# Seven quarter products for nine pairs of a gated MLP's up projection, with GpSimd forming the sums of the weights

## The chip, the cores and the metric

The kernel runs on one core of a Trainium2 chip. The metric is the device time of one execution in microseconds (us), lower is better. The engines are named as the profile names them: PE (TensorE, matrix products), DVE (VectorE), ACT (ScalarE), POOL (GpSimd) and SP (SyncE, which here only issues transfers). SBUF is the on-chip memory, PSUM the eight banks into which PE writes.

## The reference, cut to what matters

One layer of a streaming encoder over 512 tokens of width 1024: four parallel token mixers merged by gates, cross-attention into 256 memory tokens, then a gated MLP, each part between two RMS norms and added to the residual stream. All is float32. The change lies in the MLP (and in where the residual waits meanwhile):

```python
hf = _rms_norm(x, norm_ffn_pre)                       # 512 x 1024
u = _dwconv_causal(hf @ w_up, ffn_dw) + ffn_dw_b      # 512 x 5632, causal width 3 along the tokens
u_g, u_v = split(u, 2)                                # 2816 gate columns, 2816 value columns
yff = (silu(u_g) * u_v) @ w_down                      # 512 x 1024
x = x + _rms_norm(yff, norm_ffn_post)
```

## The kernel before

Every matrix product is made of three passes in a reduced float32 format. An operand is split into a high part (a cast by ACT) and a low part (operand minus high part, a subtraction by DVE); `mm3` (L239) then issues high x high, high x low and low x high into the same PSUM bank. `split_weights` (L179) does the split of a block of weights: the cast `wh` (L190, ACT) and the difference `wl` (L191, DVE). `run_blocks` (L203) takes the jobs of all stages in one line and fetches the weights three jobs ahead: the load by SP into `wr` (two buffers), then cast and difference into four buffers each. The order of the instructions on each engine is then set by the compiler's scheduler, under the waits that tiles and banks impose; each engine works its own queue in that order, and the issue of a transfer stands in the queue of the engine that issues it.

**The up projection** is `up_jobs` (L1550). There are 22 pairs j of 128 gate columns and 128 value columns. A product of 128 columns with all 512 tokens takes eight blocks of 128 input channels, three passes each: 24 matmuls with 512 columns. The tokens' operand is the tile pair `hth`, `htl`. The first four products (pairs 0 and 1) are done in two halves of 256 tokens, so that they can begin before the last tokens are normalised. After each product, ACT starts the causal convolution (`Identity` with bias and scale, L1557) and DVE adds the two other taps (L594, twice per product, one of its operands in PSUM). After the value product the gate is applied: tanh on ACT (L1561), then two operations of DVE (L1562, L1564) that write the pair's result into `quart`, the store of activations for the down projection.

**The down projection** is `down_jobs` (L1599). It already is Strassen's scheme with seven quarter products: rows of `w_down` are taken in 11 groups of two 128-row blocks, and phase 0 forms the products M1, M6, M5, M7, phase 1 the products M2, M3, M4. The sums of the weights are made while the up projection runs: `Sums` (L527) loads the rows on ACT's queue (L538), forms four sums on DVE (L542 to L545), and stores the result to DRAM on ACT's queue (L549); the down projection loads it from there (`load_parts`, L561, on SP's queue). The sums of the activations are four operations of POOL per group of two pairs (L566 to L569), issued in the up projection as soon as the second pair of the group is done, so that the down projection finds them ready.

**The residual.** `norm_task` (L1290) writes the residual of each 128 tokens into `ns.out[t]`, four tiles `res0` to `res3` of 128 x 1024 that stay in SBUF until `finish` (L1704) adds the MLP's normed result.

Of the kernel before, what the change touches and what calls it, by code (L numbers as in the profile page):

```python
# [17 lines left out]
F32 = mybir.dt.float32  # L18
# [65 lines left out]
def hybrid_layer(ctx: ExitStack, tc: tile.TileContext, a: dict, out: bass.AP):  # L84
# [146 lines left out]
    def matmul(ps, lhs, rhs, start, stop):  # L231
        PE.matmul(ps, lhs, rhs, start=start, stop=stop)  # L232
        bg.clock += max(int(math.prod(rhs.shape[1:])), 256) * 0.00042
# [293 lines left out]
    class Sums:  # L527


        def __init__(self, w, pairs, tile, queue, name):  # L530
            self.w, self.tile, self.queue, self.held = w, tile, queue, {}
            self.pairs, self.dram = pairs, dram.tile([pairs * P, 2 * D], F32, name=name)
# [7 lines left out]
        def add(self, q):  # L540
# [3 lines left out]
            V.tensor_tensor(b11, b22, b11, ALU.add)  # L544
            V.tensor_tensor(b21, b21, b11, ALU.subtract)  # L545
# [578 lines left out]
    def then(f):  # L1124

        return None, None, f
# [163 lines left out]
    def norm_task(t, ms, scaled, src, gain, act):  # L1290
# [17 lines left out]
    def open_mix_out():  # L1308
        close(m2)
        ns.res_, resp = new_pool("res", False)  # L1310
        ns.xr, ns.normed = None, []
        ns.out = [resp.tile([P, D], F32, name=f"res{t}") for t in range(NT)]
# [191 lines left out]
    def open_cross_out():  # L1504
# [5 lines left out]
        ns.hf = new_ht()  # L1510

# [26 lines left out]
    def open_ffn():  # L1538
# [6 lines left out]
        ns.quart = [(ns.fp.tile([P, 4, S // 2], F32, tag=f"qa{q}", name="qa"),  # L1545
                     ns.fp.tile([P, 3, S // 2], F32, tag=f"qb{q}", name="qb")) for q in range(NF // 2)]
        ns.post = ns.fp.tile([P, D], F32, name="g_ffn")
        G.dma_start(ns.post, a["norm_ffn_post"][0].partition_broadcast(P))

    def up_jobs():  # L1550
        st, held = {}, []

        def done(j, i, ps):
            if i == 0:
                st[j] = ns.fp.tile([P, 2, S], F32, tag="c", name="c", bufs=2)
            c, ch = st[j], i * NF + j
            st["first"] = A.activation(c[:, i], ps, AF.Identity, bias=pc("fb", ch), scale=pc("fdw2", ch)).ins  # L1557
            st["taps"] = taps(c[:, i], ps, lambda k: pc("fdw01", k * 44 + ch), 3).ins
            if i == 1:
                th = ns.fp.tile([P, S], F32, tag="th", name="th")  # L1560
                A.activation(th, c[:, 0], AF.Tanh, scale=0.5)  # L1561
                V.scalar_tensor_tensor(th, th, 1.0, c[:, 0], ALU.add, ALU.mult)  # L1562
                x = ns.quart[j // 2]
                V.scalar_tensor_tensor(x[j % 2][:, 0:2].rearrange("p a b -> p (a b)"), th, 0.5, c[:, 1],  # L1564
                                       ALU.mult, ALU.mult)
                if j % 2:
                    activation_sums(*x, G)


        for n in range(2 * NF):  # L1570
            def body(hi, lo, n=n):
                j, i = divmod(n, 2)
                if n > 3:
                    ps = bank()
                    channel_major(ps, (hi, lo), ns.hf)
                    done(j, i, ps)

                    q = n // 3 - 2
                    if 0 <= q < NF // 2:
                        with tc.issue_after(st["taps" if n % 3 == 0 else "first"]):  # L1580
                            (ns.sums.add, ns.sums.store, ns.sums.load)[n % 3](q + 2 * (n % 3 == 2))
                    return
                if n == 0:
                    bg.drain("n0")
                ps = bank(("mm", "sc")[n % 2])
                (channel_major if n else by_pass)(ps, (hi, lo), ns.hf, slice(0, S // 2))
                held.append((j, i, ps, (hi, lo)))
                if n == 3:
                    open_ffn()
# [230 lines left out]
```

## Time and profile before

| what | value |
|---|---|
| median of 3 runs | 1057.53 us (1055.94 to 1058.54) |
| the profiled execution's own time | 1055.79 us |
| its span in the profile | 1054.0 us, so 1.79 us lie around it |
| stage of the up projection | about 696 to 938 us of the span |
| stage of the down projection | about 938 us to the end |
| mean granted TensorE clock | 0.997 |

The profile shows one execution. Its page gives the busy time of each engine, the chain of work that ended last, and groups of instructions by line; the trace behind it can also be asked for the busy time of each engine in a stretch (windows) and for all instructions in order of time (timeline). In a timeline a line reads: start, duration, engine, line of the kernel, operation, output<-inputs, partitions x elements and count; a bracket at its end gives the idle time of the engine before it and what ended it. PE's matmuls overlap each other, so their spacing, not their duration, is what each costs.

### The profile page before, as it was taken

How to read it: one execution, taken by the hardware profiler on the slowest of the kernel's cores; microseconds unless marked ns; L12 is line 12 of the kernel's file. 1: busy time of each engine (PE TensorE's matmuls, PEld its weight loads, DVE VectorE, ACT ScalarE, POOL GpSimd, SP SyncE). 2: the span in 40 equal slices, each digit the busy share in tenths (PEclk: the TensorE clock that was granted, in tenths of full speed). 3: DMA queues.
4: the chain of work that ended last, by engine and by line, in shares of the span. 5: the costliest groups of instructions: out<-in, count | busy, mean ns of one | idle time of the engine just before them, and what ended most of it. 6: DMA issues, size and time to landing. Idle time of an engine off the chain costs nothing.

```text
span 1054.0 us, 14559 instructions
## 1 busy us (share of the span) xinstructions
PE 1041.7 (99%) x5295; PEld 886.8 (84%) x5295; DVE 807.1 (77%) x1280; ACT 501.9 (48%) x823; POOL 184.3 (17%) x309
## 2 busy tenths in 40 slices
PE   9999999999999999999999999999999999999996
PEld 8888888888888988888888899998888888888885
DVE  6899997668667467867487798777878777777795
ACT  5322222277465365655444566554333333355661
POOL 4000000300231233433011031121112111111001
PEclk9999999999999999999999999999999999999998
DMA  8854434742342353232359644135576676626662
GB/s 276 282 168 102 103 100 142 193 109 81 116 140 82 100 161 101 80 100 85 96 172 284 207 132 126 60 111 190 186 243 229 214 233 215 196 81 211 210 188 80
DMA packets 165373, 163.08 MB, mean 155 GB/s; under 512 B 6527, under 2 KB 136172, under 8 KB 165045
## 3 DMA queue, kind: packets, MB, share of 16 engines
q1 hardware_dynamic: 152995, 119.91, 38.0%
q0 software_dynamic: 5824, 19.03, 6.2%
q10 hardware_dynamic: 6482, 23.21, 5.7%
q8 instruction: 42, 0.69, 0.3%
q14 instruction: 30, 0.25, 0.1%
HBM read 139.03 MB, written 23.09 MB: 154 GB/s over the span
## 4 chain that ended last, share of the span: by engine, by line
PE 99%; DVE 0%; ACT 0%; issue 0%; POOL 0%; POOLq 0%; DVEq 0%; ACTq 0%
PE ps_mm L232 51%; PE ps_av L232 31%; PE ps_sc L232 8%; PE ps_tr L232 4%; PE ps_tr L236 2%; PE ps_mm L442 1%; PE ps_av L442 1%; PE ps_mm L384 0%; PE ps_sc L389 0%; DVE o L1710 0%; PE ps_tr L426 0%; POOL st_m L270 0%; POOLq L1816 0%; ACT hth L155 0%; ACT hth L432 0%
## 5 line engine op out<-in xcount | busy, mean ns | idle before, releaser
L190 ACT CAST wh<-wr 128x1024 fp32r<-128x1024 f32 (+1 forms) x142 | 148.8, 1049 | 273.3 <-PE ps_mm L232 175.0
L191 DVE TENSOR_TENSOR wl<-wr,wh 128x1024 fp32r<-128x1024 f32 (+1 forms) x142 | 178.5, 1258 | 79.0 <-ACT wh L190 78.8
L232 PE MATMUL ps_mm<-hth,wh 128*128 128x512 f32 (+1 forms) x592 | 221.1, 380 | 0.2 <-ACT hth L155 0.2
L232 PE MATMUL ps_mm<-htl,wh 128*128 128x512 f32 (+1 forms) x592 | 220.7, 379 | 0.0
L232 PE MATMUL ps_mm<-hth,wl 128*128 128x512 f32 (+1 forms) x592 | 220.6, 379 | 0.0
L232 PE MATMUL ps_av<-htl,wh 128*128 128x512 f32 (+1 forms) x352 | 131.8, 374 | 0.0
L232 PE MATMUL ps_av<-hth,wh 128*128 128x512 f32 (+1 forms) x352 | 131.8, 374 | 0.0
L232 PE MATMUL ps_av<-hth,wl 128*128 128x512 f32 (+1 forms) x352 | 131.6, 374 | 0.0
L232 PEld LDWEIGHTS ps_mm<-hth,wh 128*128 128x128 f32 x592 | 109.6, 188 | 20.4 <-ACT hth L155 0.8
L232 PEld LDWEIGHTS ps_mm<-hth,wl 128*128 128x128 f32 x592 | 109.5, 188 | 20.1
L232 PEld LDWEIGHTS ps_mm<-htl,wh 128*128 128x128 f32 x592 | 109.6, 188 | 19.7
L665 DVE SCALAR_TENSOR_TENSOR y<-y,par,y 128x482 f32<-128x482 f32 (+29 forms) x120 | 83.3, 735 | 0.1
L232 PEld LDWEIGHTS ps_av<-hth,wl 128*128 128x128 f32 x352 | 66.1, 188 | 11.9
L232 PEld LDWEIGHTS ps_av<-hth,wh 128*128 128x128 f32 x352 | 66.2, 188 | 11.8
L232 PEld LDWEIGHTS ps_av<-htl,wh 128*128 128x128 f32 x352 | 66.0, 188 | 11.7
L1613 DVE TENSOR_TENSOR wl<-dw,wh 128x1024 fp32r<-128x1024 f32 x32 | 40.2, 1262 | 13.3 <-ACT wh L1612 13.1
L1612 ACT CAST wh<-dw 128x1024 fp32r<-128x1024 f32 x32 | 33.4, 1051 | 23.4 <-PE ps_tr L232 7.9
L1058 POOL TENSOR_SCALAR fbias<-ck,cq 128x128 f32<-128x128 f32 (+3 forms) x32 | 28.2, 888 | 63.0 <-DVE st L1065 59.7
L1561 ACT ACTIVATE th<-c 128x512 f32<-128x512 f32 x22 | 13.9, 632 | 48.0 <-DVE c L594 48.0
L155 ACT CAST pth<-ps_tr 128x512 fp32r<-128x512 f32 (+3 forms) x56 | 23.5, 448 | 24.7 <-PE ps_tr L236 24.6
L594 DVE SCALAR_TENSOR_TENSOR c<-ps_mm,par,c 128x510 f32<-128x510 f32 (+1 forms) x44 | 32.8, 744 | 0.7
L156 DVE TENSOR_TENSOR ptl<-ps_tr,pth 128x512 fp32r<-128x512 f32 (+3 forms) x56 | 27.5, 512 | 5.9 <-ACT pth L155 5.4
(493 smaller groups left out, 2132.5 us busy)
## 6 DMA issues: line engine op xcount, KB each, us to landing
wr<-in_w_up SPq DMA_DIRECT2D x44, 512.0 KB
wr<-in_w_in SPq DMA_DIRECT2D x38, 512.0 KB
wr<-in_w_gate SPq DMA_DIRECT2D x32, 512.0 KB
wp<-in_w_down ACTq DMA_DIRECT2D x22, 512.0 KB
sums<-wp ACTq DMA_DIRECT2D x22, 512.0 KB
dw<-sums SPq DMA_DIRECT2D x44, 256.0 KB
wr<-in_w_branch SPq DMA_DIRECT2D x16, 512.0 KB
wide<-in_w_out SPq DMA_DIRECT2D x12, 512.0 KB
```

Of the source, the lines that this page charges most:

```text
L155: A.copy(hi, ps)
L156: V.tensor_tensor(lo, ps, hi.bitcast(F32), ALU.subtract)
L190: order(A.copy(hi, raw[:, :n]))
L191: low.tensor_tensor(lo, raw[:, :n], hi.bitcast(F32), ALU.subtract)
L232: PE.matmul(ps, lhs, rhs, start=start, stop=stop)
L236: PE.transpose(ps, x, ident[:n, :n])
L442: keep(PE.matmul(banks[c][:, :S // 2], w[p == 1][:, k, c * P:(c + 1) * P], ht[p == 2][:, i * 4 + k, :S // 2], start=(i, p, k) == (0, 0, 0) ...
L594: ins = V.scalar_tensor_tensor(dst[:, s:], src[:, :S - s], w(k), dst[:, s:], ALU.mult, ALU.add)
L665: ins = V.scalar_tensor_tensor(dst[:, s:], src[:, :S - s], pc("conv_dw", k * 4 + j), dst[:, s:], ALU.mult, ALU.add)
L1058: G.tensor_scalar(bias[:, :w], ck[j][:, :w], -1.0, cq[:, qt, head:head + 1], ALU.mult, ALU.add)
L1612: A.copy(hi, x)
L1613: V.tensor_tensor(lo, x, hi.bitcast(F32), ALU.subtract)
```

## The change

Nine of the 22 pairs (j = 4, 6, ..., 20) are computed by seven quarter products. For such a pair the matrix of [gate; value] weights (2 x 128 columns by 2 x 512 channels) is cut into four quarters, and so is the operand of the tokens (2 x 512 channels by 2 x 256 tokens). Each quarter product is four blocks of 128 channels, three passes, 256 token columns: 12 matmuls with 256 columns, 84 per pair in place of 48 with 512. Their results are combined in PSUM where the scheme allows (`x` takes A11, S2, S1 and S4 in turn, read out between them by ACT copies) and by three additions of DVE into a new tile `u`; convolution and gate then read `u` from SBUF.

- `token_terms`: once, POOL forms the four sums of the token operand's quarters, eight operations of 128 x 1024 (four add the high and low parts together again, four combine); ACT and DVE split them (`t0` to `t7`).
- `first_weights`: per pair, POOL forms four sums of weights of 128 x 512 (`su` twice, `wv` in place, `s4`). `load_pair` brings the raw weights one pair ahead into a ring of seven 128 x 1024 tiles, tag `dw`, which is shared with the tiles of `Sums` and, later, the down projection's loads. Three blocks of 128 x 1024 and one of 128 x 512 are split per pair, where it was two of 128 x 1024.
- The PE work of a pair j by seven products is laid between the halves of the plain pair j + 1, on the bank tags `sc` (two banks, for `x` and `v`) and `tr`.
- `Sums`: the last two of its four sums go to POOL (L544, L545 with `self.last`); its steps are taken by `step`, at most four per two pairs.
- The gate: `Silu` on ACT and one multiplication on DVE, in place of tanh and two operations.
- The sums of the activations move from the up projection to the down projection (`activation_terms`, POOL, three operations of 128 x 256 per group in phase 0 and one in phase 1), because `quart` now has room for the four plain quarters only; their splits become two instructions per part where they were one. The tiles that they use (`t6`, `t7`) are those of the token terms of the product A22.
- The residual is also stored to DRAM (`kept`, one transfer per 128 tokens on SP's queue), its SBUF tiles are used for token terms, and it is loaded again in `reload` at the third group of phase 0, together with the norm's gain (`ns.post`).

```diff
-            V.tensor_tensor(b11, b22, b11, ALU.add)
-            V.tensor_tensor(b21, b21, b11, ALU.subtract)
+            self.last.tensor_tensor(b11, b22, b11, ALU.add)
+            self.last.tensor_tensor(b21, b21, b11, ALU.subtract)
...
+        else:
+            SP.dma_start(ns.kept[t * P:(t + 1) * P, :], ns.out[t])
...
+    def ring(dtype=F32, name="dw"):
+        return ns.fp.tile([P, D], dtype, tag="dw", name=name, bufs=7)
+
+    def token_terms():
+        tok = [slice(i * S // 2, (i + 1) * S // 2) for i in range(2)]
+        b = {}
+        for k, t in ((0, 0), (0, 1), (1, 1), (1, 0)):
+            ks = slice(4 * k, 4 * k + 4)
+            x = b[k, t] = ring(name="b").rearrange("p (k c) -> p k c", k=4)
+            G.tensor_tensor(x, ns.hf[0][:, ks, tok[t]].bitcast(F32), ns.hf[1][:, ks, tok[t]].bitcast(F32), ALU.add)
+            if (k, t) == (0, 1):
+                G.tensor_tensor(b[0, 0], x, b[0, 0], ALU.subtract)
+            elif (k, t) == (1, 1):
+                G.tensor_tensor(b[0, 1], x, b[0, 1], ALU.subtract)
+                G.tensor_tensor(x, x, b[0, 0], ALU.subtract)
+            elif (k, t) == (1, 0):
+                G.tensor_tensor(x, x, b[1, 1], ALU.subtract)
+        for i, n in ((0, (0, 0)), (1, (1, 1)), (2, (0, 1)), (3, (1, 0))):
+            split(b[n], *ns.terms[i])
...
-                A.activation(th, c[:, 0], AF.Tanh, scale=0.5)
-                V.scalar_tensor_tensor(th, th, 1.0, c[:, 0], ALU.add, ALU.mult)
...
+            A.activation(c[:, 0], c[:, 0], AF.Silu)
+            V.tensor_tensor(ns.quart[j // 2][:, j % 2 * 2:j % 2 * 2 + 2].rearrange("p a b -> p (a b)"), c[:, 0],
+                            c[:, 1], ALU.mult)
...
+        seven = range(4, NF, 2)
...
+            def product(ps, name, b, first=True):
+                hi, lo = w[name]
+                for k in range(4):
+                    for i, (w_p, x_p) in enumerate(((hi, b[0]), (hi, b[1]), (lo, b[0]))):
+                        matmul(ps[:, :S // 2], w_p[:, k], x_p[:, k], first and i == k == 0, i == 2 and k == 3,
+                               not first)
+            def add(dst, ps):
+                V.tensor_tensor(dst, dst, ps[:, :S // 2], ALU.add)
+            def first_weights():
+                g, v = raws[j]
+                su, s4 = kept["su"], kept["s4"] = ring(name="su"), ns.fp.tile([P, S], F32, tag="s4", name="s4")
+                G.tensor_tensor(su[:, :S], v[:, :S], v[:, S:], ALU.add)
+                G.tensor_tensor(su[:, S:], su[:, :S], g[:, :S], ALU.subtract)
+                G.tensor_tensor(v[:, :S], g[:, :S], v[:, :S], ALU.subtract)
+                G.tensor_tensor(s4, g[:, S:], su[:, S:], ALU.subtract)
+                weights(("A11", "A12"), g)
+                return [()]
+            def second_weights():
+                load_pair(j + 2)
+                weights(("S1", "S2"), kept["su"])
+                return [()]
+            def third_weights():
+                weights(("S3", "A22"), raws.pop(j)[1])
...
+                split(kept["s4"], hi, lo)
...
+            def third(_):
+                u = kept["u"]
+                product(x["v"], "S3", ns.terms[2])
+                half_sums(*x["n"], range(4, NK))
+                done(n, 0, x["n"][0])
+                product(x["x"], "S1", ns.terms[0], False)
+                A.copy(u[:, 1, 1], x["x"][:, :S // 2])
+                add(u[:, 1, 1], x["v"])
+                step()
+            def value(hi, lo):
+                u, ps = kept["u"], bank()
+                half_sums(ps, (hi, lo), range(4))
+                product(x["x"], "S4", old(1, 1), False)
+                A.copy(u[:, 0, 1], x["x"][:, :S // 2])
+                half_sums(ps, (hi, lo), range(4, NK))
+                done(n, 1, ps)
+                step()
+                product(x["v"], "A22", ns.terms[3], False)
+                add(u[:, 1, 0], x["v"])
+                c = ns.fp.tile([P, 2, S], F32, tag="c", name="c", bufs=2)
+                for i in range(2):
+                    first_and_taps(c, j, i, u[:, i].rearrange("p a b -> p (a b)"))
+                gated(c, j)
+                step()
...
+        def reload():
+            ns.out = [term_tile(t).rearrange("p a b -> p (a b)") for t in range(NT)]
+            for t in range(NT):
+                SP.dma_start(ns.out[t], ns.kept[t * P:(t + 1) * P, :])
...
+            x, s = ns.quart[q], parts["terms"][phase]
+            if phase:
+                G.tensor_tensor(s[:, q % 4], x[:, 2], x[:, 1], ALU.subtract)
+                return
+            s = s[:, q % 2 * 2:q % 2 * 2 + 2]
+            G.tensor_tensor(s[:, 0], x[:, 1], x[:, 3], ALU.add)
+            G.tensor_tensor(s[:, 1], x[:, 0], x[:, 1], ALU.subtract)
+            G.tensor_tensor(x[:, 1], s[:, 0], x[:, 0], ALU.subtract)
```

More of the change, by code (lines that the diff above doesn't have):

```diff
@@ L1570, in up_jobs @@
[L1570 to L1589, printed above, removed]
-                    for j, i, ps, w in held:
-                        (channel_major if i or j else by_pass)(ps, w, ns.hf, slice(S // 2, S))
-                        done(j, i, ps)
-                    ns.sums = Sums(w_down, NF // 2, lambda: ns.fp.tile([P, D], F32, tag="dw", name="wp", bufs=4), A,
-                                   "sums")
-                    ns.sums.load(0)
-                    ns.sums.load(1)
-            yield *cols(w_up, n % 2 * DFF + n // 2 * P), body, V, same, HALF_SHIFT if n < 4 else 0
@@ new lines, in done, with sums, step, half_sums @@
+                gated(st[j], j)
+        def sums():
+            ns.sums = Sums(w_down, NF // 2, lambda: ring(name="wp"), A, "sums", G)
+            for q in range(NF // 2):
+                yield ns.sums.load, q
+                yield ns.sums.add, q
+                yield ns.sums.store, q
+        steps = sums()
+        def step():
+            f, q = next(steps, (None, None))
+            if f is not None:
+                with tc.issue_after(st["first"]):
+                    f(q)
+        def half_sums(ps, w, ks):
+            hi, lo = w
+            for k in ks:
+                mm3(ps, hi[:, k], lo[:, k], ns.hf[0][:, k], ns.hf[1][:, k], k == 0, k == NK - 1)
```

133 lines of the change are left out of this document (109 added, 24 removed).

## The prediction

> **What bounds the kernel now.** I read the page first: PE's busy share, then the chain of work that ended last. Then the windows by stage, since an average over stages says nothing of the up projection.
>
> ```profile
> span 1054.0 us, 14559 instructions
> ...
> PE 1041.7 (99%) x5295; PEld 886.8 (84%) x5295; DVE 807.1 (77%) x1280; ACT 501.9 (48%) x823; POOL 184.3 (17%) x309
> ...
> PE 99%; DVE 0%; ACT 0%; issue 0%; POOL 0%; POOLq 0%; DVEq 0%; ACTq 0%
> ```
> ```profile
> 743.70:765.50 21.80, 21.80 (x98) 18.06 (x97) 16.73 (x22) 8.21 (x11) 4.14 (x4) 1.00 0.68 222
> ...
> 932.00:940.00 8.00, 8.00 (x37) 6.59 (x36) 3.91 (x5) 4.03 (x5) 0.73 (x1) 1.00 0.32 106
> ...
> 1033.00:1054.00 21.00, 10.58 (x59) 9.05 (x57) 12.39 (x20) 3.92 (x12) 4.30 (x9) 0.85 0.27 101
> ```
>
> The columns of a window are its length, the busy us of PE, PEld, DVE, ACT and POOL, the granted clock, DMA share and GB/s. In two pairs of the up projection (first row) PE never rests; DVE is busy 16.7 of 21.8 us, ACT 8.2, POOL 4.1. At the change from up to down projection (second row) PE doesn't rest either. So time saved on PE counts in full, as long as the others keep up; the second engine is DVE.
>
> **What PE saves.** The spacing of matmuls comes from the chain, where a run of equal matmuls is one row:
>
> ```profile
> 612.22 5.65 PE ps_mm L232 x48
> ...
> 764.44 5.44 PE ps_mm L232 x24
> ```
>
> With 512 columns a matmul costs 5.44 / 24 = 0.2267 us; with 256 columns (the first row, products with the memory tokens) 5.65 / 48 = 0.1177 us, a little more than half. Nine pairs lose 9 x 48 = 432 of the first kind, 97.92 us, and gain 9 x 84 = 756 of the second, 88.98 us (the built kernel has 756 more of 256 columns). That is **-8.95 us**; of the seven-eighths saving (12.24) the narrower form takes back 3.3. Were a narrow matmul to cost 97.92 / 756 = 0.1295, nothing would be left.
>
> **What the others must now do beside it.** POOL has so far formed sums of 128 x 256. What they cost, and what they do to DVE, is in the timeline:
>
> ```profile
> 768.81 0.73 POOL L566 TENSOR_TENSOR qa<-qa,qb 128x256 f32<-128x256 f32 x1 [9.28 <-DVE qb L1564]
> ...
> 791.04 1.12 POOL L566 TENSOR_TENSOR qa<-qa,qb 128x256 f32<-128x256 f32 x1 [10.02 <-DVE qb L1564]
> 792.24 1.07 POOL L568 TENSOR_TENSOR qa<-qa 128x256 f32<-128x256 f32 x1
> 793.38 1.61 POOL L569 TENSOR_TENSOR qb<-qb,qa 128x256 f32<-128x256 f32 x1
> ...
> 8.01 1.29 POOL L415 TENSOR_TENSOR wa<-e,wa 128x512 fp32r<-128x512 f32 x1 [0.37 <-ACT wa L412]
> ```
> ```profile
> 743.57 1.23 DVE L191 TENSOR_TENSOR wl<-wr,wh 128x1024 fp32r<-128x1024 f32 x1 [0.24 <-ACT wh L190]
> 744.71 0.68 DVE L545 TENSOR_TENSOR wp<-wp 128x512 f32<-128x512 f32 x1
> ...
> 791.60 1.11 DVE L544 TENSOR_TENSOR wp<-wp 128x512 f32<-128x512 f32 x1
> 792.63 1.76 DVE L191 TENSOR_TENSOR wl<-wr,wh 128x1024 fp32r<-128x1024 f32 x1
> 794.31 1.23 DVE L545 TENSOR_TENSOR wp<-wp 128x512 f32<-128x512 f32 x1
> 795.46 1.52 DVE L594 SCALAR_TENSOR_TENSOR c<-ps_mm,par,c 128x510 f32<-128x510 f32 x2
> ```
>
> Alone a POOL sum takes 0.73, DVE's `wl` 1.23 and its 128 x 512 sum 0.68. From 791 to 795.5 both work with two operands from SBUF, and each instruction ends only after the other engine's: 0.73 becomes 1.07 to 1.61, 1.23 becomes 1.76, 0.68 becomes 1.11 and 1.23. They take turns, an instruction at a time; only some 0.14 us at an instruction's ends overlaps. The taps (L594), with one operand in PSUM, aren't slowed. The Trainium skill, "SBUF — State Buffer", section "Who interferes with whom", states this as a rule: a VectorE instruction with two SBUF inputs and a GpSimd instruction that reads SBUF exclude each other, for the whole instruction. The trace agrees (0.73 to 1.61). The rule speaks against this change, which moves sums to POOL and has DVE's taps for the nine pairs read `u` in SBUF.
>
> So I price a POOL sum by what it holds: 128 x 512 takes 1.29 and holds 1.15; 128 x 1024, by the line through 0.73 and 1.29, 2.41 (at most 4 x 0.73 = 2.9).
>
> **Steady state, two pairs.** PE needs 84 x 0.1177 + 48 x 0.2267 = 20.77 us. DVE's prices:
>
> ```profile
> L594 DVE SCALAR_TENSOR_TENSOR c<-ps_mm,par,c 128x511 f32<-128x511 f32 x14 | 10.5, 750 | 0.5
> ...
> L156 DVE TENSOR_TENSOR ptl<-ps_tr,pth 128x256 fp32r<-128x256 f32 x12 | 4.6, 412 | 0.0
> ...
> L1562 DVE SCALAR_TENSOR_TENSOR th<-th,c 128x512 f32<-128x512 f32 x14 | 9.7, 690 | 7.6 <-ACT th L1561 7.6
> ...
> L190 ACT CAST wh<-wr 128x1024 fp32r<-128x1024 f32 x28 | 29.4, 1048 | 59.2 <-PE ps_mm L232 46.6 <-PE ps_av L232 7.5 <-DMA wr<-in_w_up 5.2
> L1557 ACT ACTIVATE c<-ps_av,par 128x512 f32<-128x512 f32 x15 | 11.6, 772 | 0.0
> L1561 ACT ACTIVATE th<-c 128x512 f32<-128x512 f32 x14 | 8.9, 633 | 36.2 <-DVE c L594 36.2
> ...
> L155 ACT CAST xqh<-ps_mm 128x256 fp32r<-128x256 f32 x4 | 1.5, 366 | 2.2 <-PE ps_mm L232 2.2
> ```
>
> DVE: five `wl` 6.15, `s4l` 0.68, eight taps 6.0, three additions from PSUM (like the 412 ns row) 1.24, two gates 1.38 (four operations before), 8/3 sums 1.81: 17.3, less 0.08 overlap (743.57 + 1.23 against 744.71) for each of 21.7 instructions, 15.5. POOL: 4 + 8/3 sums, 6.67 x 1.15 = 7.7. If none blocks DVE, 15.5 of 20.77 leaves 5 us free and costs nothing; if all do, DVE needs 23.2, 2.4 too many. Of DVE's 21.7 instructions seven (four taps and the three additions, with an operand in PSUM) leave POOL alone, and a sum that starts while DVE waits on ACT blocks less: I take 0.6 of it, 20.1, just under PE. Little is left for a late wait, so I put **+2 us** on the eight steady pairs (bounds 0 and 8 x 2.4 = 19.5). ACT stays under 12 us: five casts 5.2, four of L1557 3.1, four 128 x 256 copies and one 128 x 512 cast about 2.1, two SiLU, taken like the tanh, 1.3.
>
> **The start.** The eight token sums and the first weights' sums fall together.
>
> ```profile
> 709.30 1.29 DVE L156 TENSOR_TENSOR htl<-ps_tr,hth 128x512 fp32r<-128x512 f32 x2 [2.71 <-ACT hth L155]
> ...
> 714.71 1.23 DVE L191 TENSOR_TENSOR wl<-wr,wh 128x1024 fp32r<-128x1024 f32 x1 [4.12 <-ACT wh L190]
> ...
> 720.73 0.40 PE L232 MATMUL ps_av<-hth,wh 128*128 128x512 f32 x1
> ```
>
> The last low parts of the tokens are there at 710.6; one token sum can come earlier, seven follow. Alone they'd end at 710.6 + 7 x 2.49 = 728.0. But DVE starts on its `wl` and term splits at 714.7 (1.15 each, back to back), and walking both queues in their built order, by turns, I get 730.7 for the last token sum, 739.4 for the four weight sums, 747.2 for DVE's second `Sums` operation, 750.1 for POOL's two. ACT's queue then bites: the two stores of `Sums` (issued by ACT, waiting for POOL's 750.1) stand ahead of the SiLU of pair 3 (waiting for DVE's taps, 754.3), and that ahead of the cast of the block S3|A22: 756.0. PE wants that cast after four plain products, A11 and A12, and half a gate product: 720.73 + 4 x 5.44 + 24 x 0.1177 + 12 x 0.2267 = 748.0. Stall 8 us. Without the turns the same chain ends at about 746, no stall. I take **+7** (bounds 0 and 10, the latter with 2.9 us per token sum).
>
> **Up to down.** `t6` and `t7` are free only after the last A22 product, the last PE work of the stage in the built order. From there: two POOL sums of the first group (2 x 0.82 with the gap) and a 128 x 512 cast on ACT, 620 ns by the row below, before PE's next matmul: 2.4 us at least, as no other PE work is left. The quarters that M1 needs come with POOL's fifth sum, and DVE's last taps and a `wl` take turns with these; walked, the two waits are 3.2 and 2.4. I take **+5** (bounds 2.4 and 7).
>
> ```profile
> L1612 ACT CAST n<-dw 128x512 fp32r<-128x512 f32 x11 | 6.8, 620 | 8.3 <-DMA dw<-sums 8.3
> ...
> xin<-in_x POOLq DMA_DIRECT2D x4, 512.0 KB, 6.0
> ...
> L1070 ACT ACT_TABLE_LOAD x1 | 1.3, 1283 | 0.5 <-DVE st L1068 0.5
> ```
>
> **Phase 0 of the down projection.** Per group PE has 24 x 0.2267 = 5.44 us; DVE 2 x 1.15 + 2 x 0.6 = 3.5 and three POOL sums that hold 0.6 each, four in the first groups: 5.3 to 5.9. Jobs are split three ahead: **+0.5** (bounds 0 and 4).
>
> **At nothing:** the four stores and reloads of the residual (512 KB lands in 6.0 us; the reload is needed some 80 us after its issue; the loads of `dw` queued behind it on SP are wanted over 10 us later; uncovered, 6 us); the new table load for SiLU (1.28, while ACT waits for taps; uncovered, 1.3); the longer splits of activations (ACT has over 2 us of 5.44 free).
>
> **The sum:** -8.95 + 7 + 2 + 5 + 0.5 = +5.6 us. From the profiled execution's 1055.79 that gives 1061.3; the median of the runs shown, 1057.53, lies 1.74 above that execution, so **1063 us**.
>
> **Rivals.** *The turns don't reach PE*: the scheduler's slack takes the start and the steady pairs, and only the unavoidable 2.4 us at the change of stages are paid: -8.95 + 2.4 = -6.5, 1051. For it: PE never rested in the up projection, DVE has 5 us free in two pairs. Against: the walk of the start. It decides whether the S3|A22 cast of pair 4 is done by about 748. *About even*: half of the start and 4 at the change, -8.95 + 4 + 0.5 + 4 = -0.5, 1057. *DVE is the bound in every pair*: each POOL sum blocks it, -8.95 + 8 + 19.5 + 5 = +23.6, 1081; the half of it, 1071, is nearer, as a third of DVE's instructions leave POOL alone. A long stall has a further price:
>
> ```profile
> 1043.06 0.52 PE L232 MATMUL ps_av<-dwr,a 128*128 128x256 f32 x3
> ```
>
> after PE's last matmul (1043.6) the window 1033 to 1054 shows a mean clock of 0.85, so it was halved for the last 6.3 us, from some 4 us after PE stopped. The Trainium skill ("TensorE: Matmul & The Clock Gate", "What's actually happening") puts it at one idle window of about 3.4 us, and as long a busy one to come back; by that, an estimate, the start's stall would add 1.7 us. *It saves nothing on PE*: needs 0.1295 per narrow matmul, and the 48 in a row speak against it; below 2%.
>
> **Chances.** Slower by 3 to 13 us (1061 to 1070, the forecast) 0.45; DVE the bound (1071 to 1081) 0.17; about even 0.16; the turns don't reach PE 0.22. A measurement of this kernel can tell about 0.3%, 3.2 us, from no change. So faster 0.22, same 0.16, slower 0.62. The range cuts a tenth from each end, half of the faster case and the upper part of the slowest: 1051 to 1078.
>
> **What would show it.** Step by step in the profile after: 256-column matmuls 0.118 apart; POOL's 128 x 512 sums over 1.3 us and `wl` over 1.23 where they meet; a PE wait of 5 to 8 us once, released by ACT's cast of `wv`, near 748 us; a PE wait of 2.5 us or more before the first `wr` matmul of the down projection, released through `t6`; PE otherwise busy in windows of 20.8 us. If PE shows no wait near 748, or POOL's sums don't lengthen, I am wrong on the start; if PE rests in every pair, on the steady state.

## The result, and the profile after

The changed kernel takes **1086.21 us** (median of 4 runs, 1084.86 to 1087.79) against 1057.12 before: a ratio of 1.0275, 95% interval 1.0255 to 1.0295. It is 29 us slower, above the range given. The profiled execution took 1084.86.

The page of the changed kernel: span, busy time by engine, chain that ended last.

```profile
span 1083.1 us, 15453 instructions
...
PE 1044.2 (96%) x5619; PEld 895.4 (83%) x5619; DVE 858.3 (79%) x1307; ACT 533.3 (49%) x904; POOL 315.5 (29%) x375
...
PE 74%; DVE 11%; issue 5%; DMA 4%; POOL 3%; ACT 2%; ACTq 0%; DVEq 0%; POOLq 0%; SPq 0%
```

PE falls from 99% to 96% of a longer span, and from 99% to 74% of the chain; the rest of the chain is DVE, issue (time in which an engine waited for nothing that the profile shows), transfers, POOL and ACT. No other engine is near full: DVE's share of the span rises by two points. So PE waits, and waits for several things. The waits of PE over the whole span, largest first (total us, times, longest):

```profile
PE ps_sc L232 <- ACT wh L190: 6.1, 1, 6.1
PE ps_sc L232 <- DVE u L1648: 3.4, 3, 1.2
PE ps_mm L232 <- ACT wr L1766: 2.8, 1, 2.8
PE ps_mm L232 <- DVE wl L1767: 2.1, 1, 2.1
PE ps_av L232 <- DVE wl L191: 2.1, 4, 0.8
```

One long wait (the start), one of 2.8 (up to down), one of 2.1 (phase 0), and many of about 1. Windows of the changed kernel (length, busy PE, PEld, DVE, ACT, POOL, granted clock, DMA share, GB/s): the start's stall and what follows, two steady stretches, then the first 34 us of the down projection.

```profile
748.50:754.60 6.10, 0.03 (x1) 0.00 (x0) 4.38 (x4) 1.59 (x3) 5.41 (x5) 0.82 0.54 193
754.60:765.00 10.40, 10.02 (x52) 9.11 (x53) 7.65 (x10) 4.50 (x7) 5.50 (x4) 0.78 0.87 293
...
786.00:830.00 44.00, 41.65 (x262) 36.41 (x261) 38.43 (x43) 21.64 (x32) 19.23 (x12) 1.00 0.67 219
830.00:898.00 68.00, 63.92 (x395) 55.99 (x393) 59.66 (x65) 32.12 (x48) 32.79 (x20) 1.00 0.67 214
957.00:974.00 17.00, 16.45 (x64) 12.59 (x65) 16.58 (x14) 8.74 (x14) 17.00 (x15) 0.90 0.22 64
974.00:991.00 17.00, 12.23 (x49) 8.49 (x48) 14.44 (x12) 8.32 (x12) 16.92 (x15) 1.00 0.38 123
```

PE's busy time hides slow and widely spaced matmuls, so I count its loss another way, from the timeline: the time between the starts of two matmuls, less 0.2267 us for one of 512 columns and 0.1179 for one of 256. Summed by stage, for this and for every kernel below: *start* is from the first seven-product pair to 10 us after its first product with a token sum, *steady* from there to the end of the up projection, *change* 3 us before and 6 after the first matmul of the down projection, *phase 0* the next 34, *later* the rest to the last matmul. The losses are those of the one profiled execution of each kernel, the medians those of all its runs. Each ratio is to the kernel before as it ran beside that kernel (medians 1055.73 to 1057.12), so it isn't the quotient with the first row.

| kernel | median us | ratio to before (95%) | start | steady | change | phase 0 | later |
|---|---|---|---|---|---|---|---|
| before | 1057.12 | | | | 0.1 | 0.1 | 0.0 |
| changed | 1086.21 | 1.0275 (1.0255 to 1.0295) | 8.8 | 15.2 | 5.3 | 6.8 | 1.7 |
| e1 activations' sums by DVE | 1077.85 | 1.0200 (1.0185 to 1.0215) | 9.1 | 15.8 | 4.7 | 0.0 | 0.1 |
| e2 weights' sums by DVE | 1072.93 | 1.0153 (1.0137 to 1.0168) | 5.8 | 5.9 | 6.1 | 7.5 | 0.0 |
| e3 stores by POOL | 1080.21 | 1.0219 (1.0202 to 1.0236) | 9.1 | 13.2 | 6.1 | 7.6 | 0.0 |
| e4 sums of `w_down` by DVE | 1079.57 | 1.0219 (1.0203 to 1.0234) | 6.8 | 10.5 | 5.3 | 6.8 | 0.7 |
| e5 = e1 + e2 + e4 | 1063.09 | 1.0061 (1.0040 to 1.0081) | 2.0 | 9.9 | 4.0 | 0.0 | 0.1 |
| e6 = e5 + other tiles | 1055.81 | 0.9996 (0.9986 to 1.0006) | 2.4 | 2.3 | 0.1 | 0.1 | 0.1 |
| e7 = e6, eight pairs | 1053.29 | 0.9973 (0.9961 to 0.9984) | 0.1 | 2.8 | 0.1 | 0.1 | 0.7 |
| e8 = e7 + stores by POOL | 1054.52 | 0.9980 (0.9970 to 0.9991) | 0.1 | 4.8 | 0.1 | 0.1 | 0.7 |
| e9 = e7 + idle sums 512 | 1083.64 | 1.0263 (1.0237 to 1.0289) | 6.8 | 27.4 | 0.1 | 0.1 | 0.7 |
| e10 = e7 + idle sums 128 | 1056.64 | 1.0008 (0.9999 to 1.0017) | 1.2 | 6.5 | 0.1 | 0.1 | 0.7 |
| e11 = e7, `w_down` on POOL | 1055.65 | 0.9997 (0.9988 to 1.0007) | 1.4 | 4.6 | 0.1 | 0.1 | 0.7 |
| e12 changed, eight pairs | 1084.26 | 1.0275 (1.0257 to 1.0293) | 2.1 | 19.8 | 5.3 | 6.8 | 0.9 |
| e13 = e7 + idle memsets | 1053.81 | 0.9977 (0.9966 to 0.9987) | 1.0 | 3.0 | 0.1 | 0.1 | 0.7 |
| e14 = e7 + late sums | 1055.45 | 0.9996 (0.9987 to 1.0006) | 1.7 | 5.4 | 0.1 | 0.1 | 0.1 |
| e15 = e2 + idle sums 512 | 1104.48 | 1.0453 (1.0433 to 1.0472) | 0.5 | 42.5 | 5.2 | 6.8 | 0.9 |

The changed kernel's row adds up to 37.8, before's to 0.2; with PE's saving, 432 x 0.2267 - 756 x 0.1179 = 8.8, that makes 37.8 - 0.2 - 8.8 = 28.8 of the 29.1 us between the spans. So the saving is there in full; what was underrated is the steady pairs, 15.2, and phase 0, 6.8.

What a steady wait looks like: DVE, then POOL, then PE, of the changed kernel, in one pair.

```profile
793.46 2.20 DVE L191 TENSOR_TENSOR wl<-wv,wh 128x1024 fp32r<-128x1024 f32 x1
795.59 0.74 DVE L594 SCALAR_TENSOR_TENSOR c<-ps_av,par,c 128x510 f32<-128x510 f32 x1
796.25 1.12 DVE L156 TENSOR_TENSOR s4l<-s,s4h 128x512 fp32r<-128x512 f32 x1
797.29 0.74 DVE L594 SCALAR_TENSOR_TENSOR c<-ps_av,par,c 128x511 f32<-128x511 f32 x1
797.95 1.12 DVE L594 SCALAR_TENSOR_TENSOR c<-u,par,c 128x510 f32<-128x510 f32 x1
798.99 1.77 DVE L1590 TENSOR_TENSOR qa<-c 128x512 f32<-128x512 f32 x1
800.69 1.77 DVE L594 SCALAR_TENSOR_TENSOR c<-u,par,c 128x511 f32<-128x511 f32 x1
802.38 0.41 DVE L1648 TENSOR_TENSOR u<-u,ps_sc 128x256 f32<-128x256 f32 x1
802.72 1.97 DVE L191 TENSOR_TENSOR wl<-su,wh 128x1024 fp32r<-128x1024 f32 x1
```
```profile
793.29 1.29 POOL L544 TENSOR_TENSOR wp<-wp 128x512 f32<-128x512 f32 x1 [9.83 <-DMA wv<-in_w_up]
794.54 2.28 POOL L1653 TENSOR_TENSOR su<-wv 128x512 f32<-128x512 f32 x1
796.78 1.75 POOL L545 TENSOR_TENSOR wp<-wp 128x512 f32<-128x512 f32 x1
798.48 1.74 POOL L1654 TENSOR_TENSOR su<-su,wg 128x512 f32<-128x512 f32 x1
800.18 1.73 POOL L1655 TENSOR_TENSOR wv<-wg,wv 128x512 f32<-128x512 f32 x1
801.87 1.72 POOL L1656 TENSOR_TENSOR s<-wg,su 128x512 f32<-128x512 f32 x1
```
```profile
802.85 0.50 PE L232 MATMUL ps_sc<-t,wh 128*128 128x256 f32 x2 [1.08 <-DVE u L1648]
```

POOL idles 9.83 us, then six sums come back to back, two of `w_down` and the four of the pair. From 799 on the two engines alternate, one instruction each in 1.7 us: the gate's multiplication, 0.68 alone, takes 1.77 (0.60 and a sum's 1.15), and so does the tap behind it, which reads `u` in SBUF. DVE's eight instructions from 793.46 to 802.72 would take 5.4 us by the prediction's prices less the overlap; they took 9.3. The taps from PSUM (0.74) aren't touched. At the end of this burst stands the addition at 802.38 for which PE has waited 1.1 us. Not every steady wait has this form: the next one, 1.0 us at 807.6, ends on a cast of ACT, and the chain ahead of it holds the landing of a store of `w_down`'s sums.

### The profile page after: what moved, and what is told of

Its sections match the earlier page's. It is cut to its first block, busy times and chain, and to the rows that moved or that the text cites. A ratio compares the mean times of both kernels' runs of the same rounds, so it can differ in the third digit from the quotient of the medians.

```text
span 1083.1 us, 15453 instructions
## 1 busy us (share of the span) xinstructions
PE 1044.2 (96%) x5619; PEld 895.4 (83%) x5619; DVE 858.3 (79%) x1307; ACT 533.3 (49%) x904; POOL 315.5 (29%) x375
## 4 chain that ended last, share of the span: by engine, by line
PE 74%; DVE 11%; issue 5%; DMA 4%; POOL 3%; ACT 2%; ACTq 0%; DVEq 0%; POOLq 0%; SPq 0%
PE ps_mm L232 38%; PE ps_av L232 22%; PE ps_sc L232 8%; DVE c L594 3%; PE ps_tr L232 2%; DVE wl L191 2%; PE ps_tr L236 2%; DVE qa L1590 1%; DVE wl L1767 1%; POOL t L1788 1%; DMA dw<-sums 1%; DMA dw<-in_w_down 1%; DMA wp<-in_w_down 1%; POOL t L1787 1%; DMA sums<-wp 1%
## 5 line engine op out<-in xcount | busy, mean ns | idle before, releaser
L190 ACT CAST wh<-wr 128x1024 fp32r<-128x1024 f32 (+1 forms) x124 | 129.9, 1050 | 210.7 <-PE ps_mm L232 118.3
L232 PE MATMUL ps_mm<-hth,wh 128*128 128x512 f32 (+1 forms) x520 | 193.5, 380 | 1.4 <-ACT wh L190 1.2
L232 PE MATMUL ps_mm<-hth,wl 128*128 128x512 f32 (+1 forms) x520 | 192.8, 378 | 0.8 <-DVE wl L191 0.8
L232 PE MATMUL ps_mm<-htl,wh 128*128 128x512 f32 (+1 forms) x520 | 192.9, 378 | 0.0
L232 PE MATMUL ps_av<-hth,wl 128*128 128x512 f32 (+1 forms) x280 | 104.3, 373 | 2.1 <-DVE wl L191 2.1
L232 PE MATMUL ps_av<-hth,wh 128*128 128x512 f32 (+1 forms) x280 | 103.9, 371 | 0.0
L232 PE MATMUL ps_av<-htl,wh 128*128 128x512 f32 (+1 forms) x280 | 103.9, 371 | 0.0
L232 PE MATMUL ps_sc<-t,wh 128*128 128x256 f32 x288 | 55.0, 289 | 10.5 <-ACT wh L190 6.1
L232 PEld LDWEIGHTS ps_sc<-t,wh 128*128 128x128 f32 x288 | 47.1, 194 | 15.7 <-ACT wh L190 6.5
L232 PE MATMUL ps_sc<-t,wl 128*128 128x256 f32 x144 | 41.1, 285 | 0.0
L544 POOL TENSOR_TENSOR wp<-wp 128x512 f32<-128x512 f32 x11 | 15.5, 1409 | 72.5 <-DVE wp L543 62.6
```

The costliest lines, as they stand in the source:

```text
L190: order(A.copy(hi, raw[:, :n]))
L232: PE.matmul(ps, lhs, rhs, start=start, stop=stop, skip_group_check=more)
L544: self.last.tensor_tensor(b11, b22, b11, ALU.add)
```

## The experiments

Two theories stood first. **Turns**: POOL's sums hold DVE, in the burst above. **Queue**: casts on ACT stand behind the stores of `w_down`'s sums, which wait for POOL's L545. For phase 0 the rival is DVE's **backlog**. Later a third, **late results**: POOL's sums are merely slow to arrive.

### e1: activations' sums by DVE

All four operations of `activation_terms`, of which one is shown:

```diff
-            G.tensor_tensor(s[:, 0], x[:, 1], x[:, 3], ALU.add)
+            V.tensor_tensor(s[:, 0], x[:, 1], x[:, 3], ALU.add)
...
```

> The three activation sums per group of the down projection's phase 0 (and the one of phase 1) are done by DVE instead of POOL; nothing else. The changed kernel lost about 6 us in phase 0 (PE waits of 0.4 to 2.1 us between 971 and 991 us) and 5 at the change of stages. Theory 'turns' (each POOL sum holds DVE for its own length, so that a 128 x 256 sum costs 1.15 us on both engines): DVE gains 3 x 0.35 us of work per group of 5.44 but is no longer held, so phase 0's waits fall below 2.5 us and the whole kernel comes to 1077 to 1081. Theory 'backlog' (DVE is late in phase 0 only because no split of the down projection could be made before the last up product): DVE has more to do, so 1085 to 1089.

1077.85 us, 8 less: phase 0's loss goes from 6.8 to 0.0, though DVE has more to do. Turns, not backlog. Whether PE waits for a DVE that is held, or for sums of a POOL that is held, this run doesn't tell, as it takes both away.

### e2: weights' sums by DVE

All four sums of `first_weights`, of which one is shown:

```diff
-                G.tensor_tensor(su[:, :S], v[:, :S], v[:, S:], ALU.add)
+                V.tensor_tensor(su[:, :S], v[:, :S], v[:, S:], ALU.add)
...
```

> The four sums of weights in each of the nine pairs are done by DVE instead of POOL; the sums of w_down and of activations stay on POOL. Theory 'turns': DVE's own work in two pairs grows from 15.5 to 17.9 us of 20.77, but it is no longer held by four POOL sums of 1.15 or more; the steady pairs' loss of about 13 us falls to about 4, the whole to 1075 to 1079. Theory 'queue' (the steady loss comes from ACT's queue, where casts stand behind the stores of w_down's sums, and from ring buffers that come free when those stores land): DVE is loaded more and the order stays, so 1086 to 1092.

1072.93, 13 less, better than expected; steady 15.2 to 5.9, start 8.8 to 5.8. DVE does 36 more sums, and the stage in which it does them gets faster; the change of stages and phase 0 don't (6.1 and 7.5).

### e3: stores by POOL

```diff
         def store(self, q):
             for i, x in enumerate(self.held.pop(q)):
-                self.queue.dma_start(self.dram[q * P:(q + 1) * P, i * D:(i + 1) * D], x)
+                G.dma_start(self.dram[q * P:(q + 1) * P, i * D:(i + 1) * D], x)
```

> The stores of w_down's sums are issued by POOL, which makes the last two of these sums itself, instead of ACT; so no cast on ACT stands behind them. Theory 'queue': the 5.9 us that ACT's casts waited for POOL's L545 in the steady pairs, and most of the stall of 6.3 us at the start, go: 1076 to 1081. Theory 'turns': DVE and POOL lengthen each other as before; only the start gains, 1 to 3 us: 1083 to 1086.

1080.21 lies in the window of queue, but for another reason: start stays at 9.1, steady falls by 2.0 only, and 3.1 us of the gain lie behind the issue of the last store (last section). Queue is worth some 2 us in the steady pairs of this profile; in e8 below the same edit wins nothing there.

### e4: the last two sums of `w_down` by DVE

```diff
-            ns.sums = Sums(w_down, NF // 2, lambda: ring(name="wp"), A, "sums", G)
+            ns.sums = Sums(w_down, NF // 2, lambda: ring(name="wp"), A, "sums", V)
```

> The last two of the four sums of w_down per group are made by DVE again, as in the kernel before; weights' and activations' sums stay on POOL. Theory 'turns': two of the 6.67 POOL sums per two pairs that hold DVE (a third) go and DVE gets 0.6 us for each: the steady loss falls by a third, 3 to 5 us, the start by 1 to 3: 1078 to 1082. Theory 'queue': the casts' waits behind POOL's L545 go wholly: 1074 to 1079.

1079.57: steady 4.7 less, start 2.0 less, as turns said; less than queue asked for.

### e5, e6, e7: only the token sums on POOL; other tiles; eight pairs

e5 has the edits of e1, e2 and e4. e6 adds this (and moves the norm's gain to tile 6, `z7` to 7):

```diff
-                parts["terms"] = term_tile(6), term_tile(7)
+                parts["terms"] = term_tile(2), term_tile(3)
-            ns.out = [term_tile(t).rearrange("p a b -> p (a b)") for t in range(NT)]
+            ns.out = [term_tile(t).rearrange("p a b -> p (a b)") for t in (0, 1, 4, 5)]
```

and e7 this:

```diff
-        seven = range(4, NF, 2)
+        seven = range(6, NF, 2)
```

> All sums of weights, of w_down and of activations are done by DVE (the edits of e1, e2 and e4 together); only the five token sums at the start stay on POOL. Theory 'turns': the gains of e1 (phase 0 and 1 us at the change of stages), e2 (12) and e4 (6) add up except where e2 and e4 remove the same waits, since DVE's own work is then 15.5 + 6.67 x 0.6 = 19.5 of 20.77 us in two pairs, with nothing to hold it: 1059 to 1064; PE's loss in the steady pairs at most 4 us, in phase 0 none. If instead the sum of work on DVE counts and not the turns (19.5 us is too near to 20.77): the steady loss stays at e2's 5 us or rises, 1065 to 1072.

> e5, and the first product's spare tiles are dealt out anew: the activation sums of the down projection go into the tiles of S2's token terms, which are free after the last S2 product, instead of those of A22's, the last product of the stage (the reloaded residual and two others move accordingly). If the loss at the change of stages (about 4 us) comes from waiting for these tiles, it falls to 1 or less, and the kernel to 3 or 4 us below e5. If it comes from DVE's backlog of taps and gate of the last two pairs, it stays within 1 us of e5.

> e6 with eight pairs (from pair 6) by the seven products instead of nine (from pair 4): PE does 48 x 0.2267 - 84 x 0.1177 = 1.0 us more, and token sums and first weights' sums get two pairs more of time (some 21.8 us). If the loss at the start comes from the token sums and their splits being late for pair 4, it goes but for a rest below 0.5 us, and the kernel is 1 to 4 us faster than e6; if the start has no loss left in e6, it is 1 us slower.

e5: 1063.09, in the window of turns, though steady (9.9) is above the 4 asked for. 3.4 of that is one wait of PE. PE's line in the timeline of e5, then DVE's:

```profile
792.43 0.80 PE L232 MATMUL ps_mm<-hth,wl 128*128 128x512 f32 x1 [3.37 <-DVE wl L191]
```
```profile
789.09 0.69 DVE L542 TENSOR_TENSOR wp<-wp 128x512 f32<-128x512 f32 x1 [4.08 <-DMA wp<-in_w_down]
...
791.15 1.22 DVE L191 TENSOR_TENSOR wl<-wr,wh 128x1024 fp32r<-128x1024 f32 x1
```

DVE stood 4.08 us at its next sum of `w_down`, whose load was late, with the `wl` that PE wanted in its queue behind. e5 scatters from 1059.54 to 1064.88, e6 from 1051.95 to 1058.04; whether such waits make the scatter I haven't shown. It bears on the losses, though: e5's profiled execution is its slowest (1064.88), e6's its fastest of ten (1051.95).

e6: the loss at the change of stages falls from 4.0 to 0.1: it was the wait for A22's tiles. The median falls by 7.3, more than these 3.9; the rest is open. The steady pairs' fall from 9.9 to 2.3 compares a slowest with a fastest execution and probably overstates it.

e7: the start's rest (2.4) goes, one pair's saving (1.0) with it: 1053.29, ratio 0.9973, the lowest median here. It is **faster than before** by 2.9 us, clear of its interval but only 0.3%; e8 and e13, which are made from it, lie below 1 in the same way. Of the saving of eight pairs, 8 x 0.98 = 7.8, the losses leave 7.8 - (3.8 - 0.2) = 4.2; that profile also began the stage 1.6 us later (722.3 against 720.7).

Two windows over the same stretch, of e6 and of e7, against the changed kernel's above:

```profile
786.00:895.00 109.00, 107.49 (x687) 97.43 (x686) 102.77 (x149) 57.59 (x86) 0.00 (x0) 1.00 0.75 238
```
```profile
786.00:895.00 109.00, 107.78 (x675) 96.29 (x674) 101.89 (x146) 55.59 (x84) 0.00 (x0) 1.00 0.72 227
```

DVE is busy 94% and 93% of the time and PE rests 1.5 and 1.2 us. In the changed kernel DVE is busy 88% (38.43 + 59.66 of 112) and PE rests 6.4. The load of DVE alone doesn't set the loss.

### e8: e7 with the stores by POOL

> e7 with the stores of w_down's sums issued by POOL, which has little else to do, instead of ACT. Theory 'queue': casts on ACT no longer stand behind a store that waits for DVE's sums: 2 to 4 us below e7. Theory 'turns' (ACT's order is second to DVE's load): within 1.5 us of e7, apart from the 3 us behind the last instruction that the same edit gained in e3 for no reason that either theory gives.

1054.52, 1.2 above e7, where queue asked for 2 to 4 below. Steady rises by 2.0, while 2.2 us are won behind the issue of the last store (6.3 in e7, 4.1 here). Queue falls for e7.

### e9, e10, e13: idle work on POOL

At the head of `first_weights`, in e9 (e10 with 128 columns in place of 512):

```diff
+                junk = ns.fp.tile([P, S], F32, tag="idle", name="idle")
+                for _ in range(4):
+                    G.tensor_tensor(junk[:, :512], g[:, :512], g[:, S:S + 512], ALU.add)
```

and in e13:

```diff
+                junk = ns.fp.tile([P, S], F32, tag="idle", name="idle")
+                G.tensor_tensor(junk[:, :8], g[:, :8], g[:, S:S + 8], ALU.add)
+                for _ in range(10):
+                    G.memset(junk, 0.0)
```

> e7 with work added that nothing needs: POOL adds, four times in each of the eight pairs, the two halves of the raw gate weights into a tile that nobody reads (128 x 512, as large as the weights' sums were). No result is waited for, so a loss can only come from holding other engines. Theory 'turns': DVE has 19.5 of 20.77 us in two pairs of its own, and four sums of 1.15 hold it for up to 4.6 more; 3.3 us too many for each of eight pairs if all of them meet it, 1.5 if 0.6 of them do: 1063 to 1080. Theory 'late results' (what e1, e2 and e4 won is that DVE makes a sum in 0.68 or 0.41 us and POOL in 1.29 or 0.73, so that what waits for it starts sooner): within 1.5 us of e7's 1053.3.

> e9 with idle sums of 128 x 128, a quarter of the columns. By the line through 0.73 us (256 columns) and 1.29 (512) such a sum takes 0.45 and holds about 0.3: four hold 1.2 us at most, which brings DVE from 19.5 to at most 20.7 of 20.77. Theory 'turns': a loss of 0 to 6 us against e7, and a quarter to a third of that of e9. Theory 'late results': none.

> e9 with the four idle sums of each pair replaced by ten memsets of 128 x 512 (0.52 us each in the trace, so that POOL works as long, 5.2 us) behind one sum of 128 x 8 that waits for the same load. The memsets write SBUF and read nothing. Theory 'turns by reading' (DVE's second operand and POOL's reads come through one thing): no loss beyond 1.5 us against e7, 1052 to 1056, and DVE's two-operand instructions keep 0.68 and 1.22 us. Theory 'any POOL work, or the changed order, costs': 1063 or more, as in e9.

e9: 1083.64, 30 us above e7, for 32 sums whose results nobody reads. e13: 1053.81, 0.5 above e7, for about as much work of POOL that reads nothing (30.0 us against 38.8 in the rows below). The taps that read `u` from SBUF, and POOL's group, in e9 and then in e13 (788 to 925 us):

```profile
L594 DVE SCALAR_TENSOR_TENSOR c<-u,par,c 128x510 f32<-128x510 f32 x10 | 9.5, 950 | 0.0
...
L1654 POOL TENSOR_TENSOR idle<-wg 128x512 f32<-128x512 f32 x24 | 38.8, 1615 | 89.4 <-DMA wg<-in_w_up 88.0
```
```profile
L594 DVE SCALAR_TENSOR_TENSOR c<-u,par,c 128x510 f32<-128x510 f32 x14 | 10.4, 744 | 0.0
...
L1655 POOL MEMSET idle<- 128x512 f32 x57 | 30.0, 527 | 3.3
```

950 ns against 744, and POOL's sum 1615 against 1290 alone; beside memsets nothing lengthens. So it is POOL's reading that holds DVE, not POOL being at work. The Trainium skill, "SBUF — State Buffer", section "Who interferes with whom", has both halves: a VectorE instruction with two SBUF inputs contends with a GpSimd instruction that reads SBUF, and not with one that only writes it. These runs agree.

Not all of e9's 30 us is holding. In its steady pairs no engine waits for a result of POOL, so the 27.4 there, against e7's 2.8, start from it; but some 7 of them are a slower PE behind three waits of 2 to 4 us (granted clock 0.50 from 838.7 to 844.0, 806.7 to 810.0 and 900.1 to 905.5, matmuls of 512 columns 0.43 apart). Most of the 6.8 at the start is one wait that ends at 775.1, when POOL had been idle for some 37 us; it stays open.

e10: 1056.64, 3.4 above e7, a ninth of e9's loss for a quarter of the columns: below the quarter to third that I expected. It looks as if the slack takes short holds and not long ones; no other run tests it.

### e11 and e12

e11 is e7 with e4's edit undone; e12 is the changed kernel with `range(6, NF, 2)` alone.

> e7, but the last two of the four sums of w_down stay on POOL. Theory 'turns': DVE's own work in two pairs is 17.9 us instead of 19.5, and 2.67 sums of POOL hold it for at most 3.1: 17.9 to 21.0, on both sides of e7; 1051 to 1057. A gain of more than 2 us against e7 would say that most of these sums don't meet DVE; a loss of more than 2 that all of them do, or that ACT's queue behind the stores matters.

> The changed kernel with one edit: eight pairs, from pair 6, instead of nine from pair 4; all sums on POOL. PE does 1.0 us more. Step 'start' of the prediction (the token sums on POOL come too late for pair 4, whose first wait cost 8.5 us with the slower clock behind it): that loss falls below 1.5 us, and one pair's share of the steady loss (15 / 8 = 1.9) goes: 1076 to 1079. If it is merely moved to pair 6 (POOL and DVE are late from then on): 1083 to 1087.

e11: 1055.65, 2.4 above e7: even two sums per group are cheaper on the loaded DVE. By the bound set, either all of these sums meet DVE or ACT's queue behind the stores, which now wait for POOL, matters; this run doesn't tell which.

e12: 1084.26, the same ratio as the changed kernel. The start's loss falls from 8.8 to 2.1 as asked, but the steady pairs, one fewer, lose 19.8 instead of 15.2. The time is that of the second reading, a loss that is moved and not removed. The trace bears that out only in part. Some 8 of the 19.8 lie at two waits: 1.8 us at 797.7 for a copy of ACT that stood behind a store of `w_down`'s sums, and 2.4 at 859.3, with DVE held up at a sum of `w_down` whose load was late, each with a granted clock of 0.52 to 0.54 in the 3.5 us behind. That these come from the token sums isn't shown.

### e14 and e15: late sums, and held DVE without late sums

e14 is e7 with this ahead of DVE's first sum of weights, which writes the same tile and so waits for it; e15 is e2 with e9's idle sums.

```diff
+                G.tensor_tensor(su[:, :8], g[:, :8], g[:, S:S + 8], ALU.add)
+                for _ in range(8):
+                    G.memset(su[:, :S], 0.0)
```

> e7 with DVE's sums of weights made late but not held: when the weights have landed, POOL adds 8 columns into the sums' tile and then sets half of it eight times (8 x 0.52 = 4.2 us), and DVE's first sum waits for that. In the changed kernel POOL delivers its four sums some 4 us later than DVE would. Theory 'late results are part of it': a loss of 4 us or more in the steady pairs against e7: 1057 to 1066. Theory 'turns alone': the scheduler's slack takes 4 us, within 2 us of e7.

> e2 (weights' sums on DVE, the others on POOL as in the changed kernel) with four idle sums of 128 x 512 per pair on POOL, in the place where the weights' sums stood. So POOL holds DVE as in the changed kernel, but no weights' sum is late, and DVE has 2.4 us more of its own in two pairs. Theory 'turns alone': the steady loss of e2 (6 us) returns to the changed kernel's 15 or more, as 17.9 + up to 7.7 us of DVE stand against 20.77: 1084 to 1100. Theory 'late results are most of it': within 4 us of e2's 1072.9.

e14: 1055.45, 2.2 above e7, steady 2.6 more. That lies between the two theories' bounds: late results cost something, about 2 us.

e15: 1104.48, 31.6 above e2 and above the range of either theory. No weights' sum is late, but this is not holding alone: the longest wait, 8.7 us at 759.3, is for a copy of ACT, and its queue stood behind a store that waited for POOL's sum of `w_down`, which came behind three idle sums. POOL, then ACT:

```profile
748.88 6.33 POOL L1654 TENSOR_TENSOR idle<-wg 128x512 f32<-128x512 f32 x3 [10.50 <-DMA wg<-in_w_up]
755.17 2.24 POOL L544 TENSOR_TENSOR wp<-wp 128x512 f32<-128x512 f32 x1
```
```profile
758.37 0.63 ACT L1589 ACTIVATE c<-c 128x512 f32<-128x512 f32 x1 [9.01 <-POOL wp L544]
```

With the slower PE behind it (granted clock 0.52 in the next 6 us) this is some 12 of the 42.5. The other 30, against e2's 5.9, fit holding but don't prove it, as ACT waits for POOL's sums of `w_down` elsewhere too. e9 is the cleaner test: in its steady pairs nothing waits for POOL.

## Why the prediction was wrong, point by point

- **PE's saving, 8.95**: right. It is 8.8, and shows up whole in the sum of the stages.
- **POOL and DVE take turns**: right as a mechanism, and e9 against e13 shows that it costs PE. Most of what was lost goes with POOL's sums: e5, without them, loses 16 of the changed kernel's 37.8.
- **The start, +7**: right as forecast, a wait of 6.1 released by ACT's cast, from 748.5 to 754.6. The walk is in the trace step by step: POOL's second sum of `w_down` ends at 750.9 (walked 750.1), DVE's taps at 752.9 (754.3), the cast at 754.6 (756.0). The clock follows: granted 0.82 in the stall and 0.78 in the 10 us behind it (windows above), so that the products there cost up to 2.3 us more (8.8 less waits of 6.1 and 0.4). From the Trainium skill ("TensorE: Matmul & The Clock Gate", "What's actually happening") I had worked out 1.7 for this, an estimate, and the trace comes near it. But taking it away won nothing: in e12 the pairs lost about as much more. I had added the terms as if they were independent; whether they share one engine's lag, the trace of e12 leaves open.
- **Steady pairs, +2**: this is the step that failed, with 15.2 (inside the bounds of 0 and 19.5, which I then didn't carry into the range in full). I compared sums: DVE 20.1 us against PE's 20.77, so "just under PE". The load was even lower (88% busy). What I left out is that the holds aren't spread: POOL's sums come back to back, and in such a burst DVE falls behind by 9.3 - 5.4 = 3.9 us, and PE waits at its end though over the whole stage DVE has time left. Runs in its place: DVE at 93% without holds loses 2.8 us (e7); with 32 idle sums of POOL it loses 27.4 (e9). That it is the burst, and not only the number of holds, is read from the trace: no run spreads the same sums evenly. A part is the queue: the stores issued by POOL won 2.0 (e3).
- **Up to down, +5**: right in the mechanism, as it goes with other tiles (e6), and in the number, 5.3, in part by luck. The first wait is 2.8 us (walked 3.2), released as forecast by a cast behind two sums of POOL into the tiles of A22. The second is 0.4 and not 2.4; most of the rest is a slower PE behind the first wait, granted clock 0.53 from 957.0 to 960.3, which had no term.
- **Phase 0, +0.5**: failed too, 6.8, outside its bounds of 0 and 4. I had three to four sums of 0.6 per group beside 3.5 us of DVE, 5.3 to 5.9 against 5.44, and took the lower end for covered. Both engines, in the changed kernel:

```profile
962.83 1.23 DVE L1767 TENSOR_TENSOR wr<-qa,wr 128x512 fp32r<-128x512 f32 x1
963.98 1.23 DVE L1767 TENSOR_TENSOR hth<-qa,hth 128x512 fp32r<-128x512 f32 x1
965.13 1.23 DVE L1590 TENSOR_TENSOR qa<-c 128x512 f32<-128x512 f32 x1
```
```profile
963.47 1.18 POOL L1787 TENSOR_TENSOR t<-qa 128x256 f32<-128x256 f32 x1
964.62 1.18 POOL L1788 TENSOR_TENSOR t<-qa 128x256 f32<-128x256 f32 x1
965.76 1.19 POOL L1787 TENSOR_TENSOR t<-qa 128x256 f32<-128x256 f32 x1
```

  In these rows every instruction of either engine ends 1.15 after the one before, DVE 0.6 and POOL 0.55 in turn, and no instruction of DVE passes alone. POOL is busy all 34 us (17.00 and 16.92 in the windows). The count per group was wrong as well: in these 34 us POOL made some 30 sums, while PE did 113 matmuls, 4.7 groups of 24, so there were about six sums per group and not three to four, as those of later groups and of phase 1 come early. From 954 to 987 the chain that ended last runs mostly along POOL's sums: PE waits for results of a POOL that is itself held. e1 takes the whole 6.8 away.
- **At nothing**: the residual's way and the table load cost nothing that I can find; "later" loses 1.7 more than before (1.7 against 0.0), which I had not priced and which is gone in e1, e2 and e3.
- **The rivals**: "DVE is the bound in every pair" (1071 to 1081) pointed the right way and had the right cause, but not in its form: DVE is 88% busy, and 1086 is above it because of phase 0, for which it had nothing.

The sum by steps: -8.8 + 8.8 + 15.2 + 5.3 + 6.8 + 1.7 - 0.2 = 28.8, forecast 5.6; steady pairs (13.2 too low) and phase 0 (6.3) are most of the difference of 23.2.

## What to carry to other kernels

A sum of two SBUF operands given to GpSimd beside a busy VectorE isn't free work on an idle engine: it holds a VectorE instruction that also reads two SBUF operands for nearly its own length (1.15 of 1.29 us), and here DVE did the same sum in half the time, so that taking sums back onto an engine already 88% busy won 13 us. Don't judge that an engine keeps up by comparing its total with the bound's total: look whether the holds come in a burst, and how many microseconds behind one burst leaves it. Don't add up waits as if they were independent: take one away and see whether the time comes back elsewhere, as it did in e12.

## What the runs showed of the hardware

- Idle memsets of POOL (527 ns for 128 x 512) leave DVE's two-operand instructions at 744 ns; idle sums lengthen them to 950. The rule holds for SCALAR_TENSOR_TENSOR too when both its large operands lie in SBUF, and not when one is in PSUM (0.74 in the burst).
- Where POOL issues the stores of `w_down`'s sums, the span ends sooner after the last output store is issued. That store, in the changed kernel and in e3:

```profile
1076.78 0.34 ACTq L1894 DMA_DIRECT2D out<-o  x1
```
```profile
1075.92 0.35 ACTq L1894 DMA_DIRECT2D out<-o  x1
```

  From its issue to the end of the span pass 1083.1 - 1076.8 = 6.3 us and 1079.1 - 1075.9 = 3.2. In e7 and e8 it is 6.3 and 4.1. The last stores are the same; what shortens the end is open.
